# A hybrid decoder layer on one core: clamped decays, sample outer products and wide products of the mixer scan moved between ScalarE, VectorE and GpSimd

## Chip, core and metric

The kernel runs on one core of a Trainium2 chip. The metric is the device time of one execution in microseconds; of several executions the median counts. The profile is one further execution, recorded by the hardware profiler, with its own time and its own span (first to last instruction).

## What is computed

One layer in fp32, 512 prompt tokens and 8 sample tokens (520 columns, width 1024): a half-step SwiGLU feed-forward, a mixer, a second half-step feed-forward, a final norm. The changed lines lie in the mixer. Cut to what they compute:

```python
# prompt: Mamba-2 scan in chunks of 256, 16 heads of 64, 2 groups, state 128
seg = acum[:, :, :, None] - acum[:, :, None, :]
Lm = exp(where(mask, seg, -inf))                 # decays inside a chunk
y_diag = einsum('bclsg,bclsgr,bcsgrp->bclgrp', CB, Lm, xdt)
decay_end = exp(acum[:, :, -1:] - acum)
states = einsum('bclgn,bclgr,bclgrp->bcgrpn', Bc, decay_end, xdt)
S_next = S * exp(acum[:, :, -1]) + states        # between chunks
y_off = einsum('bclgn,bcgrpn,bclgr->bclgrp', Cc, S_enter, exp(acum))
# sample: one token per sequence, 8 sequences, a state of their own
S_new = exp(dt * A) * S0 + (dt * x) outer B
y = S_new . C
# beside it: the short gated convolution
y_sc = sc_b * causal_conv3(sc_c * sc_h)
```

## The kernel before

Activations lie transposed, channels on the 128 partitions and the 520 tokens in the columns, as two halves of 260. Every fp32 product is made of three matmuls of rounded parts (hi with hi, hi with lo, lo with hi), so each block of weights that lands in a `raw` buffer is split: ScalarE copies it to `hi` (L148), VectorE subtracts to get `lo` (L149). `project()` multiplies one block of 128 columns of the input projection: 48 matmuls at L205.

The mixer has three stages. First twelve calls of `conv` (project, width-4 convolution, Silu). Then eight calls of `short(j)`, the gated convolution: three projections each (product with `rr` at L970, product at L975, convolution L979, tail columns on GpSimd L980 to L986, the wide product with `r` at L987, last product L991). Between the projections `pump()` advances two generators: `scan` four times in a round of `short`, `sample` three times. Last come the gate projections and the output projection.

`scan` takes for each of 2 groups, 2 chunks (`i`) and 2 quarters (`q`, four heads) one load of decays (`s0<-scr`, 128 x 1024, L866): eight loads in all. From it come, where `i` is 1, `ce` (exp on ScalarE L870, times C on GpSimd L871), then the clamped differences `s1` (L874, four of 128x128) and `s0` (L877, four of 128x256) on VectorE, exp on ScalarE (L878, L879), then `xd` and `xe` from transposed x (L890, L892, two each), the masks (L893, L894), the matmuls that use them (L904 to L908), the output (L910) and the state (L916, and at `i` = 1 GpSimd's L920 and VectorE's L922).

`sample` has sixteen steps (2 groups, 2 halves of the sequences, 4 blocks `j`). A step loads the state `st` (two buffers, L951), scales it on ScalarE (L953, four of 128x128), makes the outer product `up` in one buffer, `place[2]` (GpSimd L955; in the profile its name is `xs`), adds it (GpSimd L956), stores the state (L957), multiplies by C and reduces (VectorE L958, L960) and adds to x (L961).

Every engine works through its own queue in order. The order in each queue is laid down ahead of time by a planner that runs over the program with estimated costs and takes, of what is ready, what stands first in the program. All loads and stores of this stage are issued from SyncE's queue, in order too.

Of the kernel before, what the change touches and what calls it, by code (L numbers as in the profile page):

```python
# [10 lines left out]
F32 = mybir.dt.float32  # L11
F32R = mybir.dt.float32r
AF = mybir.ActivationFunctionType
ALU = mybir.AluOpType
AX = mybir.AxisListType

P = 128
# [9 lines left out]
HD = 64  # L27
NG = 2
NS = 128
# [644 lines left out]
def mixer(c, o, x, nxt, nx2):  # L674
    nc, tc, a = c.nc, c.tc, c.a
    V, S, G, PE = c.V, c.S, c.G, c.PE
# [9 lines left out]
    with ExitStack() as c0:  # L686
# [28 lines left out]
        place = [t[:, :SEQ].rearrange("p (b n) -> p b n", n=NS) for t in (xst[0][:, 6], xst[0][:, 7], xst[1][:, 6])]  # L715
# [3 lines left out]
        dt = mx.tile([P, NT, NH], F32, name="dt")  # L719
        acs = mx.tile([P, NCH, NH], F32, name="acs")  # L720
# [121 lines left out]
        def scan(sp):  # L842
            states = {}
            for g in range(NG):
                Bt, Ct = xs[8 + g], xs[10 + g]
                for i in range(NC2):
                    l0 = i * 2 * P
                    both, sec = slice(l0, l0 + 2 * P), slice(l0 + P, l0 + 2 * P)
                    blk = [slice(l0, l0 + P), sec]

                    pcb = c.bank()
                    PE.matmul(pcb[:, :2 * P], Bt[:, blk[0]], Ct[:, both], start=True, stop=True)
                    PE.matmul(pcb[:, 2 * P:3 * P], Bt[:, blk[1]], Ct[:, sec], start=True, stop=True)
                    cbm = sp.tile([P, 3 * P], F32, tag="cbm", name="cbm")
                    V.tensor_tensor(cbm, pcb[:, :3 * P], tri.rearrange("p t l -> p (t l)"), op=ALU.mult)
                    pbt = c.bank()
                    for b in range(2):
                        PE.transpose(pbt[:, b * P:(b + 1) * P], Bt[:, blk[b]], idn)
                    btk = sp.tile([P, 2, P], F32, tag="btk", name="btk")
                    S.copy(btk.rearrange("p b n -> p (b n)"), pbt[:, :2 * P])  # L860
                    for q in range(2):
                        hs = slice(g * 8 + q * 4, g * 8 + q * 4 + 4)
                        js = [g * 4 + q * 2, g * 4 + q * 2 + 1]

                        s0 = sp.tile([P, 4, 2 * P], F32, tag="s0", name="s0", bufs=2)
                        nc.sync.dma_start(s0, scr[hs, both].unsqueeze(0).broadcast_to([P, 4, 2 * P]))  # L866
                        s1 = sp.tile([P, 4, P], F32, tag="s1", name="s1", bufs=2)
                        if i:
                            ce = sp.tile([P, 4, 2 * P], F32, tag="ce", name="ce")
                            S.activation(ce, s0, AF.Exp)  # L870
                            G.tensor_tensor(ce, ce, Ct[:, both].unsqueeze(1).broadcast_to([P, 4, 2 * P]), op=ALU.mult)  # L871
                        for h in range(4):
                            hc = g * 8 + q * 4 + h
                            V.tensor_scalar(s1[:, h], s0[:, h, P:], acs[:, 2 * i + 1, hc:hc + 1], 0.0, op0=ALU.subtract, op1=ALU.min)  # L874
                        for h in range(4):
                            hc = g * 8 + q * 4 + h
                            V.tensor_scalar(s0[:, h], s0[:, h], acs[:, 2 * i, hc:hc + 1], 0.0, op0=ALU.subtract, op1=ALU.min)  # L877
                        S.activation(s0, s0, AF.Exp)  # L878
                        S.activation(s1, s1, AF.Exp)  # L879
                        yield  # L880

                        px = c.bank()
                        for b in range(2):
                            for n, j in enumerate(js):
                                PE.transpose(px[:, (2 * b + n) * P:(2 * b + n + 1) * P], xs[j][:, blk[b]], idn)
                        xd = sp.tile([P, 2, 4, HD], F32, tag="xd", name="xd")
                        xe = sp.tile([P, 2, 4, HD], F32, tag="xe", name="xe")
                        for b in range(2):
                            t = 2 * i + b
                            V.tensor_tensor(xd[:, b], px[:, b * 2 * P:(b + 1) * 2 * P].rearrange("p (h d) -> p h d", d=HD),  # L890
                                            dt[:, t, hs].unsqueeze(2).broadcast_to([P, 4, HD]), op=ALU.mult)
                            V.tensor_tensor(xe[:, b], xd[:, b], dec[:, t, hs].unsqueeze(2).broadcast_to([P, 4, HD]), op=ALU.mult)  # L892
                        V.tensor_tensor(s0, s0, cbm[:, :2 * P].unsqueeze(1).broadcast_to([P, 4, 2 * P]), op=ALU.mult)  # L893
                        V.tensor_tensor(s1, s1, cbm[:, 2 * P:].unsqueeze(1).broadcast_to([P, 4, P]), op=ALU.mult)  # L894
                        yield
                        py = c.bank()
                        sin = states.get((g, q))
                        for n in range(2):
                            for step in range(3 if i else 2):
                                for h in (2 * n, 2 * n + 1):  # L900
                                    rows = slice((h % 2) * HD, (h % 2 + 1) * HD)
                                    full = py[rows, n * 2 * P:(n + 1) * 2 * P]
                                    if step == 0:
                                        PE.matmul(full, xd[:, 0, h, :], s0[:, h, :], start=True, stop=False)  # L904
                                    elif step == 1:
                                        PE.matmul(py[rows, n * 2 * P + P:(n + 1) * 2 * P], xd[:, 1, h, :], s1[:, h, :], start=False, stop=not i)
                                    else:
                                        PE.matmul(full, sin[:, h * HD:(h + 1) * HD], ce[:, h, :], start=False, stop=True)  # L908
                        for n, j in enumerate(js):
                            V.scalar_tensor_tensor(xs[j][:, both], xs[j][:, both], par("dsk", j), py[:, n * 2 * P:(n + 1) * 2 * P],  # L910
                                                   op0=ALU.mult, op1=ALU.add)
                        yield

                        pst = c.bank()
                        for b in range(2):
                            PE.matmul(pst[:, :2 * P], btk[:, b], xe[:, b].rearrange("p h d -> p (h d)"), start=b == 0, stop=b == 1)  # L916
                        sn = sp.tile([P, 2 * P], F32, tag=f"st{i}{q}", name="sn")
                        if i:
                            tm = sp.tile([P, 2 * P], F32, tag="tm", name="tm")
                            G.tensor_tensor(tm.rearrange("p (h d) -> p h d", d=HD), sin.rearrange("p (h d) -> p h d", d=HD),  # L920
                                            cd[:, i, hs].unsqueeze(2).broadcast_to([P, 4, HD]), op=ALU.mult)
                            V.tensor_tensor(sn, pst[:, :2 * P], tm, op=ALU.add)  # L922
                            nc.sync.dma_start(o["sp"][g][:, q * 2 * P:(q + 1) * 2 * P], sn)
                        else:
                            S.copy(sn, pst[:, :2 * P])
                        states[g, q] = sn
                        yield


        def sample(sd):  # L930
            pbc = c.bank()
            for n in range(4):
                PE.transpose(pbc[:NB, n * NS:(n + 1) * NS], xs[8 + n][:, SEQ:], idn)
            HB = NB // 2
            bcs = place[2][:NB]
            V.tensor_copy(bcs.rearrange("b t n -> b (t n)"), pbc[:NB])
            scb = c.dram.tile([4, NB, NS], F32, name="scb")
            nc.sync.dma_start(scb.rearrange("t b n -> b t n"), bcs)
            for g in range(NG):
                for k in range(2):  # L940
# [5 lines left out]
                    for j in range(g * 4, g * 4 + 4):  # L946
# [2 lines left out]
                        G.tensor_tensor(xd, xb, ddc[:, j, 0, bs], op=ALU.mult)  # L949
                        st = sd.tile([P, HB, NS], F32, tag="st", name="st", bufs=2)  # L950
                        nc.sync.dma_start(st, a["ssm0"][j][:, bs])  # L951
                        for b in range(HB):
                            S.activation(st[:, b], st[:, b], AF.Copy, scale=ddc[:, j, 1, k * HB + b:k * HB + b + 1])  # L953
                        up = place[2]
                        G.tensor_tensor(up, bb, xd.unsqueeze(2).broadcast_to([P, HB, NS]), op=ALU.mult)  # L955
                        G.tensor_tensor(st, st, up, op=ALU.add)  # L956
                        nc.sync.dma_start(o["ss"][j][:, bs], st)  # L957
                        V.tensor_tensor(up, st, cc, op=ALU.mult)  # L958
                        ys = sd.tile([P, HB], F32, tag="ys", name="ys", bufs=2)
# [7 lines left out]
        def short(j, pump):  # L967
# [16 lines left out]
            for k in range(1, SW):  # L984
                G.tensor_scalar(tmp, ssv[:, j, k], w[k], None, op0=ALU.mult)
                G.tensor_tensor(t1[:, SEQ:], t1[:, SEQ:], tmp, op=ALU.add)  # L986
            G.tensor_tensor(t1, t1, r, op=ALU.mult)  # L987
            pump()
            pbx = project()
            y = ytp.tile([P, T], F32, tag=f"yt{j}", name=f"yt{j}")  # L990
# [144 lines left out]
```

## Time and profile before

| | |
|---|---|
| median of three timed executions | 1176.18 us (1172.96 to 1177.44) |
| the profiled execution | 1172.36 us, its span 1170.6 us |
| mean granted TensorE clock | 0.988 of full speed |
| busy share of the span | TensorE 96%, VectorE 74%, ScalarE 44%, GpSimd 19% |

The profile calls the engines PE (TensorE matmul), PEld (its weight loads), DVE (VectorE), ACT (ScalarE), POOL (GpSimd) and SP (SyncE; a q behind a name is its queue). A row of the timeline merges like instructions that follow each other; their durations overlap by some tens of nanoseconds, so four of them can take less than four times one. Names of tiles are those of the program; several tiles that share a buffer have the name of the first.

### The profile page before, as it was taken

The numbers are of one execution on the slowest core, as the hardware profiler recorded it, in microseconds if no ns is written. First come the engines' busy times: TensorE is split into PE (matmuls) and PEld (weight loads), VectorE is DVE, ScalarE is ACT, GpSimd is POOL, SyncE is SP. The second block draws the span as 40 slices with busy tenths as digits, with TensorE's granted clock in tenths as the row PEclk, the third lists the DMA queues.
The fourth block names the chain that finished last, engine by engine and source line by source line (L and its number), as shares of the span: only waits on it lengthen the run. The fifth ranks groups of instructions, "written<-read, shape, count | busy, mean of one in ns | idle before, by whom it ended". The sixth has DMA issues, their size and how long they took to land.

```text
span 1170.6 us, 21766 instructions
## 1 busy us (share of the span) xinstructions
PE 1123.9 (96%) x9119; PEld 1101.7 (94%) x9119; DVE 871.6 (74%) x1279; ACT 514.4 (44%) x731; POOL 224.6 (19%) x301
## 2 busy tenths in 40 slices
PE   8999999999999999987899999999899999999995
PEld 7989999999999999976799999999799999999994
DVE  7987787778766687788876576348787777786855
ACT  5553444444436574334332344334554444444442
POOL 4000000000003567566643222120000000000002
PEclk9999999999999999999999999999999999999998
DMA  6213322332324433465442322331132223323233
GB/s 199 94 50 113 113 100 66 111 136 77 113 64 135 119 110 97 138 191 164 160 133 79 96 90 72 110 109 50 60 113 91 86 89 110 113 100 112 78 87 74
DMA packets 47434, 122.97 MB, mean 105 GB/s; under 512 B 9384, under 2 KB 19784, under 8 KB 41832
## 3 DMA queue, kind: packets, MB, share of 16 engines
q1 hardware_dynamic: 47336, 121.58, 31.9%
q8 instruction: 71, 1.16, 0.4%
q14 instruction: 27, 0.22, 0.1%
HBM read 114.43 MB, written 7.14 MB: 104 GB/s over the span
## 4 chain that ended last, share of the span: by engine, by line
PE 80%; DVE 6%; POOL 4%; issue 3%; DMA 3%; ACT 3%; SPq 0%; DVEq 0%; POOLq 0%; ACTq 0%
PE pst L221 32%; PE mmt L205 21%; PE auxt L576 20%; PE pst L256 3%; DVE lo L149 2%; POOL xs L955 1%; POOL st L956 1%; ACT hi L148 1%; DMA st<-in_ssm 1%; DMA raw<-in_wu 1%; DMA out_ss<-st 1%; PE auxt L904 0%; DVE y L666 0%; DVE xxl L339 0%; POOL ce L871 0%
## 5 line engine op out<-in xcount | busy, mean ns | idle before, releaser
L148 ACT CAST hi<-raw 128x1024 fp32r<-128x1024 f32 (+3 forms) x218 | 188.5, 869 | 292.8 <-PE mmt L205 105.7
L149 DVE TENSOR_TENSOR lo<-raw,hi 128x1024 fp32r<-128x1024 f32 (+3 forms) x218 | 227.0, 1044 | 60.5 <-ACT hi L148 57.6
L576 PE MATMUL auxt<-hh,hi 128*128 128x260 f32 x704 | 197.7, 283 | 0.8 <-DVE x L577 0.8
L576 PE MATMUL auxt<-hl,hi 128*128 128x260 f32 x704 | 197.5, 283 | 0.0
L576 PE MATMUL auxt<-hh,lo 128*128 128x260 f32 x704 | 194.9, 283 | 0.0
L205 PE MATMUL mmt<-xxh,hi 128*128 128x260 f32 x704 | 146.5, 289 | 0.0
L205 PE MATMUL mmt<-xxl,hi 128*128 128x260 f32 x704 | 143.8, 285 | 0.0
L205 PE MATMUL mmt<-xxh,lo 128*128 128x260 f32 x704 | 143.6, 286 | 0.0
L295 POOL TENSOR_TENSOR acc<-x 128x520 f32<-128x520 f32 x4 | 4.2, 1054 | 697.2 <-DVE x L577 674.9
L576 PEld LDWEIGHTS auxt<-hh,hi 128*128 128x128 f32 x704 | 132.2, 188 | 1.7 <-DVE x L577 0.9
L576 PEld LDWEIGHTS auxt<-hl,hi 128*128 128x128 f32 x704 | 132.5, 188 | 0.0
L576 PEld LDWEIGHTS auxt<-hh,lo 128*128 128x128 f32 x704 | 130.9, 188 | 0.1
L205 PEld LDWEIGHTS mmt<-xxh,hi 128*128 128x128 f32 x704 | 110.2, 190 | 0.6
L205 PEld LDWEIGHTS mmt<-xxl,hi 128*128 128x128 f32 x704 | 110.0, 190 | 0.3 <-issue 0.2
L205 PEld LDWEIGHTS mmt<-xxh,lo 128*128 128x128 f32 x704 | 110.0, 191 | 0.1
L148 ACT CAST hi<-S 128x1024 fp32r<-128x1024 f32 x78 | 80.8, 1050 | 66.6 <-PE pst L221 43.0
L149 DVE TENSOR_TENSOR lo<-S,hi 128x1024 fp32r<-128x1024 f32 x78 | 94.4, 1218 | 19.6 <-ACT hi L148 19.3
L386 ACT ACTIVATE cp<-pst 128x260 f32<-128x260 f32 x117 | 44.8, 386 | 122.0 <-PE pst L221 121.6
L221 PE MATMUL pst<-fxl,hi 128*128 128x260 f32 x320 | 90.2, 283 | 1.4 <-DVE fxl L286 1.4
L221 PE MATMUL pst<-fxh,hi 128*128 128x260 f32 x320 | 90.7, 286 | 0.8 <-ACT hi L148 0.4
L221 PE MATMUL pst<-fxh,lo 128*128 128x260 f32 x320 | 89.2, 283 | 1.0 <-DVE lo L149 1.0
L221 PE MATMUL pst<-fth,hi 128*128 128x260 f32 x304 | 85.7, 285 | 1.3 <-ACT hi L148 0.7
(245 smaller groups left out, 2843.6 us busy)
## 6 DMA issues: line engine op xcount, KB each, us to landing
raw<-in_wi SPq DMA_DIRECT2D x45, 512.0 KB, 3.5
raw<-in_wu SPq DMA_DIRECT2D x22, 1024.0 KB, 4.9
raw<-in_wg SPq DMA_DIRECT2D x21, 1024.0 KB, 4.8
raw<-in_wd SPq DMA_DIRECT2D x48, 384.0 KB, 3.2
raw<-in_wo SPq DMA_DIRECT2D x16, 512.0 KB, 3.8
raw<-in_wd SPq DMA_DIRECT2D x16, 256.0 KB, 2.7
st<-in_ssm SPq DMA_DIRECT2D x16, 256.0 KB, 2.9
s<-scr SPq DMA_DIRECT2D x8, 512.0 KB, 4.7
```

The source lines that it names most:

```text
L148: self.S.copy(hi, src)
L149: self.V.tensor_tensor(lo, src, hi.bitcast(F32), op=ALU.subtract)
L205: self.PE.matmul(ps[:, h, :H2], w[:, k, :], x[:, h * H2:(h + 1) * H2], start=first and n == 0, stop=last and n == 2)
L221: self.PE.matmul(ps[:, :H2], a[:, k, :], b, start=first and k + i == 0, stop=k == n - 1 and i == 2, skip_group_check=True)
L256: self.PE.matmul(ps[h][:, :H2], a, b[:, h * H2:(h + 1) * H2], start=first and n == 0, stop=last and n == 2)
L295: self.G.tensor_tensor(acc, xt, xt, op=ALU.mult)
L386: self.c.S.activation(t, ps[:, :H2], AF.Copy, scale=sign)
L576: PE.matmul(ps[:, :H2], w[:, k, :], v, start=k + n == 0, stop=k == nk - 1 and n == 2)
L955: G.tensor_tensor(up, bb, xd.unsqueeze(2).broadcast_to([P, HB, NS]), op=ALU.mult)
L956: G.tensor_tensor(st, st, up, op=ALU.add)
```

## The change

The clamp min(s - a, 0) becomes relu(a - s) on ScalarE, and the sign goes into the exp behind it. GpSimd's products for `ce`, for the carried state and with `r` go to VectorE. `xd` and `xe` are made by one instruction each instead of two. In `sample`, ScalarE makes the outer product, four instructions with a scale per partition, into one of two buffers, and VectorE scales the state and adds in one pass, four instructions. GpSimd keeps `xd` of the sample (128x4), the tail columns and the small convolution work.

```diff
-  G.tensor_tensor(ce, ce, Ct[:, both]..., op=ALU.mult)
+  V.tensor_tensor(ce, ce, Ct[:, both]..., op=ALU.mult)
   for h in range(4):
-    V.tensor_scalar(s1[:, h], s0[:, h, P:], acs[:, 2*i+1, hc:hc+1], 0.0, op0=ALU.subtract, op1=ALU.min)
+    S.activation(s1[:, h], s0[:, h, P:], AF.Relu, bias=acs[:, 2*i+1, hc:hc+1], scale=-1.0)
   for h in range(4):
-    V.tensor_scalar(s0[:, h], s0[:, h], acs[:, 2*i, hc:hc+1], 0.0, op0=ALU.subtract, op1=ALU.min)
-  S.activation(s0, s0, AF.Exp)
-  S.activation(s1, s1, AF.Exp)
+    S.activation(s0[:, h], s0[:, h], AF.Relu, bias=acs[:, 2*i, hc:hc+1], scale=-1.0)
+  S.activation(s0, s0, AF.Exp, scale=-1.0)
+  S.activation(s1, s1, AF.Exp, scale=-1.0)
...
-  for b in range(2):
-    V.tensor_tensor(xd[:, b], px[...], dt[:, 2*i+b, hs]..., op=ALU.mult)
-    V.tensor_tensor(xe[:, b], xd[:, b], dec[:, 2*i+b, hs]..., op=ALU.mult)
+  V.tensor_tensor(xd, px.rearrange("p (b h d) -> p b h d", b=2, d=HD), wide4(dt), op=ALU.mult)
+  V.tensor_tensor(xe, xd, wide4(dec), op=ALU.mult)
...
-  G.tensor_tensor(tm, sin, cd[:, i, hs]..., op=ALU.mult)
-  V.tensor_tensor(sn, pst[:, :2 * P], tm, op=ALU.add)
+  V.tensor_tensor(sn, sin, cd[:, i, hs]..., op=ALU.mult)
+  V.tensor_tensor(sn, pst[:, :2 * P], sn, op=ALU.add)
...
+  place.append(sd.tile([P, HB, NS], F32, name="up"))
...
+  up = place[2 + j % 2]
   for b in range(HB):
-    S.activation(st[:, b], st[:, b], AF.Copy, scale=ddc[:, j, 1, ...])
-  up = place[2]
-  G.tensor_tensor(up, bb, xd.unsqueeze(2).broadcast_to([P, HB, NS]), op=ALU.mult)
-  G.tensor_tensor(st, st, up, op=ALU.add)
+    S.activation(up[:, b], bb[:, b], AF.Copy, scale=xd[:, b:b + 1])
+  for b in range(HB):
+    V.scalar_tensor_tensor(st[:, b], st[:, b], ddc[:, j, 1, ...], up[:, b], op0=ALU.mult, op1=ALU.add)
...
-  G.tensor_tensor(t1, t1, r, op=ALU.mult)
+  V.tensor_tensor(t1, t1, r, op=ALU.mult)
```

## Rows read from the trace of the kernel before

**Rows 1.** Windows of convolutions, of scan with sample, of the scan's rest.

```profile
360.00:465.00 105.00, 103.06 (x824) 101.40 (x823) 76.07 (x137) 64.64 (x89) 65.68 (x134) 0.97 0.38 116
465.00:600.00 135.00, 118.86 (x943) 111.33 (x942) 116.45 (x179) 51.93 (x98) 86.74 (x97) 0.96 0.49 158
600.00:655.00 55.00, 55.00 (x459) 52.09 (x458) 35.49 (x58) 14.91 (x19) 16.31 (x25) 1.00 0.34 103
```

**Rows 2.** TensorE's waits, 465 to 655 us: total us, times, longest us.

```profile
PE auxt L904 <- DVE xd L890: 11.5, 4, 7.0
```

**Rows 3.** Timeline of TensorE behind its longest wait: start, us, instructions.

```profile
553.94 1.12 PE L904 MATMUL auxt<-s,xd 128*64 128x256 f32 x4 [7.02 <-DVE xd L890]
...
559.40 0.59 PE L205 MATMUL mmt<-xxh,hi 128*128 128x260 f32 x2
```

**Rows 4.** Timeline of VectorE in the 18 us ahead of that matmul.

```profile
536.87 3.74 DVE L877 TENSOR_SCALAR s<-s,acs 128x256 f32<-128x256 f32 x4 [1.28 <-ACT ce L870]
...
541.91 3.02 DVE L877 TENSOR_SCALAR s<-s,acs 128x256 f32<-128x256 f32 x4
...
551.66 0.69 DVE L958 TENSOR_TENSOR xs<-st,xs 128x512 f32<-128x512 f32 x1 [1.36 <-POOL st L956]
```

**Rows 5.** Timeline of GpSimd in the same stretch.

```profile
536.91 2.41 POOL L871 TENSOR_TENSOR ce<-ce,xs 128x1024 f32<-128x1024 f32 x1 [1.89 <-ACT ce L870]
...
542.07 1.08 POOL L955 TENSOR_TENSOR xs<-xs,xd 128x512 f32<-128x512 f32 x1 [2.13 <-DVE ys L960]
```

**Rows 6.** The same clamps on VectorE while GpSimd is idle, timeline.

```profile
595.09 1.13 DVE L877 TENSOR_SCALAR s<-s,acs 128x256 f32<-128x256 f32 x4
...
610.65 0.87 DVE L874 TENSOR_SCALAR s<-s,acs 128x128 f32<-128x128 f32 x4 [2.46 <-DMA s<-scr]
```

**Rows 7.** Groups on VectorE, 465 to 655 us: busy, mean ns, idle before.

```profile
L877 DVE TENSOR_SCALAR s<-s,acs 128x256 f32<-128x256 f32 x24 | 17.4, 785 | 1.3 <-ACT ce L870 1.3
...
L958 DVE TENSOR_TENSOR xs<-st,xs 128x512 f32<-128x512 f32 x16 | 12.1, 754 | 10.2 <-POOL st L956 10.1
...
L893 DVE TENSOR_TENSOR s<-s,cbm 128x1024 f32<-128x1024 f32 x8 | 9.7, 1216 | 1.2 <-ACT s L878 1.2
L874 DVE TENSOR_SCALAR s<-s,acs 128x128 f32<-128x128 f32 x24 | 9.5, 456 | 4.4 <-DMA s<-scr 4.4
L961 DVE SCALAR_TENSOR_TENSOR xs<-xs,pc,ys 128x4 f32<-128x4 f32 x16 | 9.4, 585 | 0.1
...
L890 DVE TENSOR_TENSOR xd<-auxt,dt 128x256 f32<-128x256 f32 x16 | 6.0, 412 | 0.0
L975 DVE TENSOR_TENSOR u<-mmt,t 128x520 f32<-128x520 f32 x8 | 5.5, 693 | 6.2 <-PE mmt L205 6.2
```

**Rows 8.** Two lines of VectorE by themselves: duration ns min/median/max.

```profile
L961 DVE SCALAR_TENSOR_TENSOR xs<-xs,pc,ys x16: 209/498/1119, 483.7 to 595.0; 128x4 f32<-128x4 f32 x16
...
L979 DVE SCALAR_TENSOR_TENSOR t<-u,pc,t x16: 737/747/1776, 475.4 to 644.6; 128x512 f32<-128x512 f32 x16
```

**Rows 9.** Groups on GpSimd, 465 to 655 us, as in Rows 7.

```profile
L955 POOL TENSOR_TENSOR xs<-xs,xd 128x512 f32<-128x512 f32 x16 | 25.5, 1593 | 27.4 <-DVE ys L960 26.6 <-DMA xs<-scb 0.8
L956 POOL TENSOR_TENSOR st<-st,xs 128x512 f32<-128x512 f32 x16 | 21.1, 1318 | 1.1
L987 POOL TENSOR_TENSOR t<-t,r 128x520 f32<-128x520 f32 x8 | 12.4, 1548 | 1.7 <-DVE t L979 1.7
...
L871 POOL TENSOR_TENSOR ce<-ce,xs 128x1024 f32<-128x1024 f32 x4 | 9.6, 2394 | 5.5 <-ACT ce L870 5.5
```

**Rows 10.** Groups on ScalarE, 465 to 655 us, as in Rows 7.

```profile
L953 ACT ACTIVATE st<-st,ddc 128x128 f32<-128x128 f32 x56 | 18.0, 390 | 36.1 <-DMA st<-in_ssm 34.7 <-issue 1.4
...
L977 ACT ACTIVATE t<-u,pc 128x512 f32<-128x512 f32 x8 | 5.8, 721 | 6.4 <-DVE u L975 6.4
```

**Rows 11.** Transfers issued from 465 to 600 us: KB each, us to landing.

```profile
out_ss<-st SPq DMA_DIRECT2D x16, 256.0 KB, 2.6
st<-in_ssm SPq DMA_DIRECT2D x14, 256.0 KB, 2.7
```

More of the change, by code (lines that the diff above doesn't have):

```diff
@@ L870, in scan @@
                             S.activation(ce, s0, AF.Exp)
-                            G.tensor_tensor(ce, ce, Ct[:, both].unsqueeze(1).broadcast_to([P, 4, 2 * P]), op=ALU.mult)
+                            V.tensor_tensor(ce, ce, Ct[:, both].unsqueeze(1).broadcast_to([P, 4, 2 * P]), op=ALU.mult)
                         for h in range(4):
                             hc = g * 8 + q * 4 + h
-                            V.tensor_scalar(s1[:, h], s0[:, h, P:], acs[:, 2 * i + 1, hc:hc + 1], 0.0, op0=ALU.subtract, op1=ALU.min)
+                            S.activation(s1[:, h], s0[:, h, P:], AF.Relu, bias=acs[:, 2 * i + 1, hc:hc + 1], scale=-1.0)
                         for h in range(4):
                             hc = g * 8 + q * 4 + h
-                            V.tensor_scalar(s0[:, h], s0[:, h], acs[:, 2 * i, hc:hc + 1], 0.0, op0=ALU.subtract, op1=ALU.min)
-                        S.activation(s0, s0, AF.Exp)
-                        S.activation(s1, s1, AF.Exp)
+                            S.activation(s0[:, h], s0[:, h], AF.Relu, bias=acs[:, 2 * i, hc:hc + 1], scale=-1.0)
+                        S.activation(s0, s0, AF.Exp, scale=-1.0)
+                        S.activation(s1, s1, AF.Exp, scale=-1.0)
                         yield
@@ L887, in scan @@
                         xe = sp.tile([P, 2, 4, HD], F32, tag="xe", name="xe")
-                        for b in range(2):
[L889 to L892, printed above, removed]
+                        ts = slice(2 * i, 2 * i + 2)
+                        wide4 = lambda t: t[:, ts, hs].unsqueeze(3).broadcast_to([P, 2, 4, HD])
+                        V.tensor_tensor(xd, px.rearrange("p (b h d) -> p b h d", b=2, d=HD), wide4(dt), op=ALU.mult)
+                        V.tensor_tensor(xe, xd, wide4(dec), op=ALU.mult)
                         V.tensor_tensor(s0, s0, cbm[:, :2 * P].unsqueeze(1).broadcast_to([P, 4, 2 * P]), op=ALU.mult)
@@ L918, in scan @@
                         if i:
-                            tm = sp.tile([P, 2 * P], F32, tag="tm", name="tm")
-                            G.tensor_tensor(tm.rearrange("p (h d) -> p h d", d=HD), sin.rearrange("p (h d) -> p h d", d=HD),
+                            V.tensor_tensor(sn.rearrange("p (h d) -> p h d", d=HD), sin.rearrange("p (h d) -> p h d", d=HD),
                                             cd[:, i, hs].unsqueeze(2).broadcast_to([P, 4, HD]), op=ALU.mult)
-                            V.tensor_tensor(sn, pst[:, :2 * P], tm, op=ALU.add)
+                            V.tensor_tensor(sn, pst[:, :2 * P], sn, op=ALU.add)
                             nc.sync.dma_start(o["sp"][g][:, q * 2 * P:(q + 1) * 2 * P], sn)
@@ L951, in sample @@
                         nc.sync.dma_start(st, a["ssm0"][j][:, bs])
+                        up = place[2 + j % 2]
                         for b in range(HB):
-                            S.activation(st[:, b], st[:, b], AF.Copy, scale=ddc[:, j, 1, k * HB + b:k * HB + b + 1])
-                        up = place[2]
-                        G.tensor_tensor(up, bb, xd.unsqueeze(2).broadcast_to([P, HB, NS]), op=ALU.mult)
-                        G.tensor_tensor(st, st, up, op=ALU.add)
+                            S.activation(up[:, b], bb[:, b], AF.Copy, scale=xd[:, b:b + 1])
+                        for b in range(HB):
+                            V.scalar_tensor_tensor(st[:, b], st[:, b], ddc[:, j, 1, k * HB + b:k * HB + b + 1], up[:, b],
+                                                   op0=ALU.mult, op1=ALU.add)
                         nc.sync.dma_start(o["ss"][j][:, bs], st)
```

## The prediction

> **What bounds the kernel now.** I read the page's busy shares first, then TensorE's waits, then windows around them, then the timelines of the engines it waits for. TensorE is the bound nearly everywhere, so only what takes time from it counts. The windows show where the changed lines could matter [rows 1]: with the convolutions it is busy 103 of 105 us, in the last part of the scan 55 of 55, but from 465 to 600 us, where `sample` runs beside `scan`, only 118.86 of 135. That leaves 16.1 us idle. The clock granted there is 0.96 of full: with two levels, 2.4 and 1.2 GHz, a shortfall of 0.04 is 8% of 135 us, or 10.8 us, at the low one, so at most half of it, 5.4 us, is lost besides. The timeline behind the longest wait shows such a piece [rows 3]: the scan's matmuls from 553.94 to 559.40 us follow the wait, and 5.46 us at the low level lose at most 2.7. Between 2.7 and 5.4 I take 3.5. The ceiling of what the change can give back is 16.1 + 3.5 = 19.6 us.
>
> The waits say for whom: L904 waits for VectorE's `xd` (L890) four times, 11.5 us in all, 7.0 at the longest [rows 2]. VectorE is busy 116.45 of these 135 us [rows 1] and stands another 10.1 us waiting for GpSimd's L956 [rows 7]: it is full, and its queue reaches `xd` late.
>
> Its timeline ahead of the longest wait shows what fills it [rows 4]. Four clamps L877 take 3.74 us, and a second four 3.02; with GpSimd idle four take 1.13 [rows 6]. GpSimd was at the same time in L871 for 2.41 us, then in L955 [rows 5]. So a wide GpSimd instruction holds VectorE's. That made 2.61 + 1.89 us, and with the wait of 1.36 for L956 [rows 4] 5.9 of the 7.0 us.
>
> **The change part by part**, in VectorE time of 465 to 655 us, where six of the eight decay loads and all sixteen sample steps are.
>
> Removed. The clamps: 17.4 + 9.5 = 26.9 us [rows 7]; free they would take 6 x (1.13 + 0.87) = 12.0 [rows 6], so 14.9 of it is being held. The wait for L956: 10.1 us [rows 7], since VectorE now adds the state itself. L961 takes 9.4 us for sixteen [rows 7], its shortest 0.209 [rows 8], so 9.4 - 3.3 = 6.1 is being held. The wide products that leave GpSimd are 25.5 + 21.1 + 12.4 + 9.6 = 68.6 us [rows 9] of its 86.74 + 16.31 = 103 [rows 1], two thirds, and I let two thirds of 6.1 go, 4.1. `xd` and `xe` were 32 instructions of 0.412; sixteen of double width at the 0.693 of L975, which reads PSUM too, make 11.1 in place of 13.2 [rows 7], 2.1 less. Together 43.2 us.
>
> Added. Sixty-four scale-and-add instructions of 128x128. The trace has none; the same operation takes 0.209 us for 4 columns and 0.737 for 512 [rows 8], which bound them between 13.4 and 47.2 us. On the line between the two, 128 columns take 0.209 + 124 x 0.528 / 508 = 0.338, and 64 make 21.6; I take that, as one operation should grow evenly. The product with `r`: 8 x 0.693 = 5.5. `ce`: 4 x 1.216 (L893, equal in shape) = 4.9. The carried state: 4 x 0.412 = 1.6 [rows 7]. Together 33.6 us.
>
> Relief: 43.2 - 33.6 = 9.6 us, from -16.0 (all at 0.737) to 17.8 (all at 0.209). Rows of like instructions overlap: 24 of L877 at 0.785 would be 18.8, and 17.4 are busy [rows 7], 0.06 each. The new rows of four have 48 such places: 2.9 more. So VectorE gains about 12.5 us in a stage where it was the one that was late.
>
> Moved to ScalarE. For each load four relus of 128 columns, at 0.390 by L953, and four of 256, between that and the 0.721 of L977 for 512 [rows 10], 0.50 on the line: 3.6 us a load, 21.4 for six. ScalarE is busy 51.93 of 135 us [rows 1]; the outer product replaces the scaling of the state one for one, and the eight scalings that ran ahead of this stage (64 less 56) come into it, 3.1. That makes 76 of 135, so I cost it at nothing, its idle time being the cover. Were that gone, the `hi` copies behind the relus would be late by up to 3.6 us a load. The other two loads fall among the convolutions: 7.2 us more on 64.64 of 105, nothing again, 7.2 at worst.
>
> For the relus the row and the Trainium skill pull apart. Its page "ScalarE: Activation LUTs", section "Rules for kernel authors", says to give relu, max and min to VectorE. By its rule the clamps would stay: 2.0 us a load there against 3.6. What VectorE takes with GpSimd beside it is 26.9 / 6 = 4.5 a load, and by that the sum is better with ScalarE.
>
> Waits that change places. The four adds of a sample step wait on VectorE for the load of `st`; it was ScalarE, with 34.7 us of such waits [rows 10]. Behind them in VectorE's queue stand `lo` and `xd`, for which TensorE waits. A buffer's round is store 2.6, load 2.7 [rows 11] and adds 1.4, or 6.7, so two buffers allow a step each 3.4 us, and 135 us for sixteen give each 8.4. The load should then be there, and I cost this at 0.5, as two or three of sixteen may be short by some tenths. The product with `r` now waits on VectorE for GpSimd's tail columns. There GpSimd waited 1.7 us over the eight for VectorE's L979 [rows 9], so the tail was done no later; from nothing to 8 x 1.55, I take nothing. SyncE's queue has as many transfers as before, and its stores wait for one engine less.
>
> **Sum.** 12.5 - 0.5 = 12 us of the ceiling of 19.6. Against the profiled execution, 1172.36 us with its span of 1170.6, that is 1160.4. The median of the runs is 3.8 above it, and I count from that: 1176.2 - 12 = 1164.
>
> **Rivals.** (a) VectorE stays full. If the new instruction costs the 0.412 of a 128x256 product and doesn't overlap, relief is 9.6 - 4.8 = 4.8 us: 1171. For it: two thirds of GpSimd's time gone is not all, and its small instructions still hold VectorE. Against it: L961's shortest is half of 0.412 [rows 8].
>
> (b) The relus lengthen the way from the load to the masks. If L893 and L894 come later by the 1.6 us more than free clamps, six times, 9.6 of the 12 go: 1174. By the rule in the Trainium skill's page "ScalarE: Activation LUTs", section "Rules for kernel authors", it would come out so. Against it: the clamps do not run free now.
>
> (c) The planner, given other costs, lays the queues so that TensorE meets `xd` as late as before. The order is then the cause, not the holding: 1176, give or take 5. For it: 10 us of slack in an engine do not help an instruction that stands behind the wrong one. Against it: 5.9 of 7.0 us were traced to GpSimd.
>
> (d) Slower: VectorE inherits ScalarE's waits for `st`. From 12.5 of the 34.7 us on, all relief is gone; with half of them, 17.4, it is 1181, with all 1198. For it: an engine in order passes its wait on to everything behind. Against it: the round of 6.7 us for two steps.
>
> **Chances.** The forecast 0.60, its own range 1157 to 1169; (a) 0.12, (b) 0.08, (c) 0.10, (d) 0.10. I take 0.5%, 5.9 us, as what the runs can tell from nothing, since the three shown spread over 4.5. Faster than that is the forecast with half of (a), 0.06, a quarter of (b), 0.02, and 0.03 of (c): 0.71. Within it: the rest of (a) and (b), 0.12, and 0.05 of (c): 0.17. Slower: (d) and 0.02 of (c): 0.12. The range runs from the ceiling, 1156.6, less a spread of 1.6, to 1179, which takes in (a), (b) and most of (c), and leaves out (d).
>
> **What would show it.** In the changed profile TensorE should be busy more than 125 of the stage's time for the same matmuls, and its waits for L890 under half of 11.5 us. L961 should come near 0.21 us, the adds near 0.34, and ScalarE's relus near 0.39 and 0.50. GpSimd's busy time between 465 and 655 us should fall from 103 to about 35. VectorE should wait little for `st` or for GpSimd's tail. I would be wrong if VectorE's waits for the loads of `st` go over 12 us, or the adds over 0.5, or if TensorE waits as long as before at another line.

## The result and the profile after

The changed kernel takes 1157.1 us (median of four, 1155.4 to 1158.34) against 1174.94 before (now also of four): ratio 0.9847, interval 0.9827 to 0.9867. That is 17.8 us less, where 12 were forecast; 1164 was forecast, with 1155 to 1179 as the range. The two profiled executions have spans of 1170.6 and 1153.6 us.

Windows of the changed kernel over the same three stretches as [rows 1]; the columns are the stretch, its length, busy us and instructions of TensorE, its weight loads, VectorE, ScalarE and GpSimd, then granted clock, DMA share and GB/s:

```profile
360.00:465.00 105.00, 102.18 (x840) 100.42 (x839) 70.41 (x120) 70.32 (x99) 63.74 (x133) 1.00 0.38 116
465.00:600.00 135.00, 131.28 (x1082) 125.21 (x1080) 119.42 (x225) 73.11 (x158) 34.09 (x63) 1.00 0.56 177
600.00:655.00 55.00, 55.00 (x461) 52.86 (x460) 33.86 (x46) 21.02 (x28) 10.62 (x17) 1.00 0.28 88
```

From 465 to 600 us TensorE is now idle for 3.7 us, where it was 16.1, and its clock there went from 0.96 to 1.00, the full level. VectorE is busier than before, 119.4 us against 116.45. The stage itself can be measured from the scan's first matmul (L852) to its last (L916, now L915):

```profile
L852 PE MATMUL auxt<-xs x8: 378/379/380, 464.6 to 595.7; 128*128 128x256 f32 x8
...
L915 PE MATMUL auxt<-xe,btk x32: 377/379/484, 480.4 to 632.7; 128*128 128x256 f32 x32
```

464.6 to 632.7 is 168.1 us. Before it ran from 465.0 to 650.0, 185.0. So 16.9 of the 17.0 us by which the spans differ come from this stage. Its windows, before and after, say what they consist of:

```profile
465.00:650.00 185.00, 168.86 (x1359) 158.45 (x1357) 150.04 (x232) 64.89 (x113) 103.05 (x122) 0.97 0.45 142
464.60:632.70 168.10, 164.38 (x1359) 156.15 (x1357) 140.50 (x252) 84.02 (x172) 39.88 (x76) 1.00 0.50 158
```

TensorE's idle time fell from 16.1 to 3.7 us, 12.4 less, and the same matmuls kept it busy for 164.4 us in place of 168.9, 4.5 less. The convolutions' clock also rose, 0.97 to 1.00, but TensorE was idle longer there (2.8 us against 1.9), and the stage began only 0.4 us sooner.

TensorE's waits between 360 and 760 us; the 11.5 us for `xd` [rows 2] are 0.5 now:

```profile
PE auxt L915 <- DVE xe L891: 1.1, 1, 1.1
PE auxt L885 <- ACT btk L860: 1.0, 1, 1.0
PE auxt L931 <- DVE cbm L855: 0.9, 1, 0.9
PE auxt L903 <- DVE xd L890: 0.5, 1, 0.5
```

VectorE's groups, 465 to 655 us, as in [rows 7] (L955 is now the add of the state):

```profile
L149 DVE TENSOR_TENSOR lo<-raw,hi 128x1024 fp32r<-128x1024 f32 x28 | 34.1, 1218 | 5.9 <-ACT hi L148 5.2
L979 DVE SCALAR_TENSOR_TENSOR t<-u,pc,t 128x512 f32<-128x512 f32 x16 | 11.9, 746 | 0.1
...
L955 DVE SCALAR_TENSOR_TENSOR st<-st,ddc,xs 128x128 f32<-128x128 f32 x32 | 9.7, 346 | 6.1 <-ACT xs L953 5.3 <-DMA st<-in_ssm 0.7
L955 DVE SCALAR_TENSOR_TENSOR st<-st,ddc,up 128x128 f32<-128x128 f32 x32 | 9.7, 346 | 1.3 <-ACT up L953 0.7 <-issue 0.6
...
L871 DVE TENSOR_TENSOR ce<-ce,xs 128x1024 f32<-128x1024 f32 x4 | 4.9, 1216 | 0.0
L961 DVE SCALAR_TENSOR_TENSOR xs<-xs,pc,ys 128x4 f32<-128x4 f32 x16 | 3.3, 214 | 0.0
```

The adds take 0.346 us each (0.338 was estimated). L961 fell from 0.585 to 0.214, near its shortest before, 0.209 [rows 8]. From 465 to 640 us no group of VectorE's varies by more than 6% from its shortest to its longest any more, so nothing there is held. It does wait for ScalarE's outer product, 5.3 + 0.7 us; for the load of `st` it waits 0.7.

On GpSimd the small columns remain [rows 9], and on ScalarE the relus stand beside the outer products [rows 10]:

```profile
L985 POOL TENSOR_SCALAR tmp<-ssv,pc 128x8 f32<-128x8 f32 x14 | 14.8, 1054 | 1.4
L986 POOL TENSOR_TENSOR t<-t,tmp 128x8 f32<-128x8 f32 x16 | 7.2, 450 | 1.3
```

```profile
L877 ACT ACTIVATE s<-s,acs 128x256 f32<-128x256 f32 x24 | 10.3, 496 | 0.1
L953 ACT ACTIVATE xs<-xs,xd 128x128 f32<-128x128 f32 x32 | 10.2, 390 | 10.6 <-DMA xs<-scb 6.4 <-DVE ys L960 4.2
...
L874 ACT ACTIVATE s<-s,acs 128x128 f32<-128x128 f32 x24 | 7.8, 390 | 16.4 <-DMA s<-scr 16.4
```

The relus cost what was forecast, 0.390 and 0.496 us, but ScalarE waits 16.4 us in front of them for the decays' loads. The timeline of ScalarE shows what stands behind such a wait:

```profile
511.57 0.99 ACT L874 ACTIVATE s<-s,acs 128x128 f32<-128x128 f32 x3 [6.83 <-DMA s<-scr]
512.46 1.26 ACT L953 ACTIVATE xs<-xs,xd 128x128 f32<-128x128 f32 x4
...
514.60 1.03 ACT L148 CAST hi<-raw 128x1024 fp32r<-128x1024 f32 x1
...
516.71 0.35 ACT L860 COPY btk<-auxt 128x256 f32<-128x256 f32 x1
```

An outer product, a `hi` copy and `btk` come after the 6.83 us. VectorE's add started at 512.89 after an idle 2.50 us that the product ended, and TensorE's L885 at 517.11 after 0.98 that `btk` ended.

### The profile page after: what moved, and what is told of

Its sections match the earlier page's. It is cut to its first block, busy times and chain, and to the rows that moved or that the text cites. A ratio compares the mean times of both kernels' runs of the same rounds, so it can differ in the third digit from the quotient of the medians.

```text
span 1153.6 us, 21775 instructions
## 1 busy us (share of the span) xinstructions
PE 1116.7 (97%) x9119; PEld 1095.4 (95%) x9119; DVE 854.1 (74%) x1279; ACT 538.0 (47%) x797; POOL 158.9 (14%) x253
## 3 DMA queue, kind: packets, MB, share of 16 engines
q1 hardware_dynamic: 47336, 121.58, 32.4%
## 4 chain that ended last, share of the span: by engine, by line
PE 75%; DVE 9%; DMA 6%; ACT 5%; issue 2%; POOL 2%; SPq 1%; DVEq 0%; ACTq 0%; POOLq 0%
PE pst L221 32%; PE auxt L576 20%; PE mmt L205 17%; PE pst L256 4%; DVE lo L149 2%; DMA s<-scr 2%; ACT hi L148 1%; DMA raw<-in_wu 1%; DMA out_ss<-st 1%; DVE st L955 1%; DVE cv L830 1%; DMA st<-in_ssm 1%; ACT s L874 0%; DVE r L313 0%; PE auxt L915 0%
## 5 line engine op out<-in xcount | busy, mean ns | idle before, releaser
L149 DVE TENSOR_TENSOR lo<-raw,hi 128x1024 fp32r<-128x1024 f32 (+3 forms) x218 | 222.5, 1023 | 69.8 <-ACT hi L148 66.6
L149 DVE TENSOR_TENSOR lo<-S,hi 128x1024 fp32r<-128x1024 f32 x78 | 94.4, 1218 | 19.2 <-ACT hi L148 18.7
```

The source lines that it names most:

```text
L149: self.V.tensor_tensor(lo, src, hi.bitcast(F32), op=ALU.subtract)
```

## The experiments

Theory H: a wide GpSimd instruction holds VectorE's, whichever stands next, and the change gains by taking such instructions away. Theory L: only the sum of VectorE's work counts. Theory C: the gain is the shorter chain of a sample step (a second buffer, no GpSimd in it).

**One part of the change alone, on the kernel before.** `relu_only` has the ScalarE clamps only:

```diff
-  V.tensor_scalar(s0[:, h], s0[:, h], acs[...], 0.0, op0=ALU.subtract, op1=ALU.min)
+  S.activation(s0[:, h], s0[:, h], AF.Relu, bias=acs[...], scale=-1.0)
...                                          # the same for s1, and scale=-1.0 in the exps
```

> The kernel before with the clamps alone moved to ScalarE as relus. Theory H (a wide GpSimd instruction holds VectorE's, whichever stands next): GpSimd's 68.6 us of wide products stay, so the holding passes from the clamps to other instructions of VectorE (L961, L979 and L149 grow longer than before), the wait for L956 stays near 10 us, and about half of the 17 us is gained: 1164 to 1170. Theory L (only the sum of VectorE's work counts): 26.9 us leave VectorE and nothing is added, more than the whole change relieves, so all of the gain: 1155 to 1159.

1168.16 us, ratio 0.9941 (0.992 to 0.9961). The time is as H said, and the holding passed on, though only in part where H put it. L961 grew from 0.585 to 0.921, and the wait for L956, which was to stay near 10.1, went to 16.1. L979 and L149, which were to grow too, fell to 0.810 and 1.320; the masks grew instead (L893 1.216 to 1.329). VectorE's groups, 465 to 655 us:

```profile
L961 DVE SCALAR_TENSOR_TENSOR xs<-xs,pc,ys 128x4 f32<-128x4 f32 x16 | 14.7, 921 | 0.3
...
L958 DVE TENSOR_TENSOR xs<-st,xs 128x512 f32<-128x512 f32 x16 | 12.1, 756 | 16.1 <-POOL st L956 16.1
```

`sample_only` has the sample part only (its second buffer lies in the square's scratch tile, idle in this stage):

```diff
-  S.activation(st[:, b], st[:, b], AF.Copy, scale=ddc[...])
-  G.tensor_tensor(up, bb, xd...broadcast_to([P, HB, NS]), op=ALU.mult)
-  G.tensor_tensor(st, st, up, op=ALU.add)
+  S.activation(up[:, b], bb[:, b], AF.Copy, scale=xd[:, b:b + 1])
+  V.scalar_tensor_tensor(st[:, b], st[:, b], ddc[...], up[:, b], op0=ALU.mult, op1=ALU.add)
```

> The kernel before with the sample part alone changed (outer product on ScalarE, scale-and-add on VectorE, a second buffer for the product). Theory H: 46.6 of GpSimd's 68.6 us of wide products and the wait of 10.1 us for L956 go, clamps run near their free 1.13 and 0.87 us a load except beside L871 and L987; two thirds of the gain: 1160 to 1166. Theory L: 19 to 22 us are added to VectorE and 10 us of waiting leave it, the clamps stay at 26.9, so no gain: 1174 to 1180.

1156.39 us, 0.9847 (0.9815 to 0.9879): all of the gain by itself, more than H said, against L. Its window:

```profile
465.00:600.00 135.00, 132.75 (x1098) 127.01 (x1097) 127.23 (x266) 58.34 (x112) 45.46 (x78) 1.00 0.54 174
```

`wide_only` has `ce`, the carried state and the product with `r` on VectorE:

```diff
-  G.tensor_tensor(t1, t1, r, op=ALU.mult)
+  V.tensor_tensor(t1, t1, r, op=ALU.mult)
...                                          # the same for ce and the carried state
```

> The kernel before with only the products for ce, the carried state and r moved from GpSimd to VectorE. Theory H: 25 us of GpSimd's wide work go, a third of the holding, some 8 to 10 us, against 12 us of work added to VectorE: no change, 1171 to 1178. Theory L: 12 us more on a full engine, 1180 to 1188.

1167.38 us, 0.9935 (0.9912 to 0.9957). Faster, where H expected no change and L a loss, so a miss for both: VectorE got more work (121.58 us busy from 465 to 600, 116.45 before), and TensorE was idle for 9.0 us in place of 16.1.

**One part of the change undone.** `no_sample` keeps relus, VectorE's products and the fused `xd` and `xe`, with `sample` as before.

```diff
-  S.activation(up[:, b], bb[:, b], AF.Copy, scale=xd[:, b:b + 1])
-  V.scalar_tensor_tensor(st[:, b], st[:, b], ddc[...], up[:, b], op0=ALU.mult, op1=ALU.add)
+  S.activation(st[:, b], st[:, b], AF.Copy, scale=ddc[...])
+  G.tensor_tensor(up, bb, xd...broadcast_to([P, HB, NS]), op=ALU.mult)
+  G.tensor_tensor(st, st, up, op=ALU.add)
```

> The changed kernel with the sample part as before (GpSimd makes and adds the outer product, one buffer); relus, VectorE's products and the fused xd and xe stay. Theory H: 46.6 us of wide GpSimd work and the wait for L956 stay, 22 are gone; with the clamps off VectorE it has room, 1162 to 1168. If the parts simply added (6.9 for the relus, 7.7 for the products), 1160.

1170.73 us, 0.9967 (0.9948 to 0.9985): a miss for both figures. The two parts that gained 6.9 and 7.7 us alone gain some 4 together, with the fused `xd` and `xe` besides. The windows, of 465 to 600 us and of the stage from its first L852 to its last L915, are the plainest case against L. VectorE is busy 140.59 us of the stage, where the changed kernel has 140.50, yet the stage lasts 181.1 us and not 168.1, and TensorE is idle for 12.2. VectorE's waits at the sample step, 9.9 us for GpSimd's add against 6.7 in the changed kernel, account for 3 of these 13 us at most.

```profile
465.00:600.00 135.00, 122.85 (x976) 116.23 (x975) 111.97 (x150) 66.72 (x141) 76.89 (x100) 0.96 0.53 168
464.50:645.60 181.10, 168.95 (x1357) 159.42 (x1356) 140.59 (x188) 82.48 (x164) 82.89 (x114) 0.97 0.47 147
```

`no_relu` keeps all but the clamps, which go back to VectorE; `no_relu_again` is the same file beside the changed kernel, `after_again`, in one session.

```diff
-  S.activation(s0[:, h], s0[:, h], AF.Relu, bias=acs[...], scale=-1.0)
+  V.tensor_scalar(s0[:, h], s0[:, h], acs[...], 0.0, op0=ALU.subtract, op1=ALU.min)
```

> The changed kernel with the clamps back on VectorE. Theory H: nothing wide is left on GpSimd, so the clamps run free, 2.0 us a load, 12 us more on VectorE in the 135 us of scan with sample, where it is busy 119: full again but not held; 2 to 6 us of the gain go: 1159 to 1163. Theory L: VectorE's 12 us come back as 12 us: 1169. The rule of the page ScalarE: Activation LUTs (clamps belong on VectorE) would have it at 1157 or under.

> The changed kernel with the clamps back on VectorE, once more. If the clamps on ScalarE cost something once nothing wide runs on GpSimd (TensorE waited 3.7 us in the scan with them and not at all without): 1150 to 1154, its ratio below that of the changed kernel beside it. If the 5 us between them was chance: 1155 to 1159.

> The changed kernel once more, on the same chip as the one with the clamps on VectorE: 1155 to 1159 by every theory.

1151.93 us, 0.9815 (0.9787 to 0.9844), then 1152.22, 0.9823 (0.9804 to 0.9843); the changed kernel beside the second 1155.19, 0.9849 (0.9831 to 0.9867). The intervals against the kernel before overlap, but the single runs do not: those without relus lie at 1150.39 to 1154.56 and 1151.15 to 1153.43, those with them at 1155.4 to 1158.34 and 1154.67 to 1156.01. So the relus cost 3 to 5 us, where H expected the clamps on VectorE to cost 2 to 6: a miss for H in its sign. The planner also lays the queues in another order without them, and no run separates the two. The window of `no_relu` has no idle time of TensorE at all, with VectorE 127 us busy, and the clamps run at their free price (the second window is the stage):

```profile
465.00:600.00 135.00, 135.00 (x1120) 129.42 (x1119) 127.44 (x268) 59.55 (x114) 38.93 (x66) 1.00 0.55 177
464.20:627.90 163.70, 163.70 (x1358) 155.95 (x1357) 147.43 (x296) 67.39 (x121) 43.55 (x74) 1.00 0.50 161
```

```profile
L149 DVE TENSOR_TENSOR lo<-raw,hi 128x1024 fp32r<-128x1024 f32 x28 | 34.1, 1218 | 1.7 <-ACT hi L148 1.1
...
L955 DVE SCALAR_TENSOR_TENSOR st<-st,ddc,xs 128x128 f32<-128x128 f32 x32 | 9.8, 344 | 1.7 <-ACT xs L953 1.7
...
L877 DVE TENSOR_SCALAR s<-s,acs 128x256 f32<-128x256 f32 x24 | 7.3, 346 | 0.0
...
L874 DVE TENSOR_SCALAR s<-s,acs 128x128 f32<-128x128 f32 x24 | 5.4, 279 | 3.4 <-DMA s<-scr 3.4
```

**The buffer.** `two_up` gives the kernel before a second buffer for the outer product; `one_up` takes it from the changed kernel.

```diff
-  up = place[2]
+  up = place[2 + j % 2]                    # two_up; one_up has it the other way
```

> The kernel before with a second buffer for the outer product of sample and nothing else. Theory H: GpSimd does the same wide work, so the holding stays: 1171 to 1178. Theory C: GpSimd's next product no longer waits for VectorE's reduction (26.6 us of such waits before), and half or more of the 17 us is gained: 1158 to 1167.

> The changed kernel with one buffer for the outer product in place of two. Theory H: nothing holds VectorE, so little changes, 1156 to 1160. Theory C: ScalarE's product waits for VectorE's reduction each step and VectorE for the product: 1164 to 1172.

1172.64 us, 0.999 (0.9972 to 1.0008), and 1158.95, 0.9853 (0.9811 to 0.9896), each within what H expected. No effect of the buffer shows either way, and C, as far as it rests on it, falls.

**Holding put back.** `held` adds idle work to the changed kernel that changes no output; `beside` is the same work tied to the step:

```diff
+  for _ in range(2):                       # per sample step, over a scratch tile of zeros
+      G.tensor_tensor(idle, idle, idle, op=ALU.mult)                   # held
+      G.tensor_tensor(idle, idle, xd...broadcast_to(...), op=ALU.mult) # beside
```

> The changed kernel with idle work added: two products of 128x512 on GpSimd at each of the sixteen sample steps, over a scratch tile that nothing reads. Theory H (a wide GpSimd instruction holds VectorE's that read two tensors or clamp): no dependence is added, but 32 x 1.05 = 34 us of wide work are back, half of what was removed; L961 and L979 grow longer again, TensorE waits for VectorE again, 1161 to 1168. Theory C (what was removed is the chain of a sample step through one buffer and through GpSimd): the chain is unchanged, so 1155 to 1159.

1166.7 us, 0.9941 (0.9917 to 0.9965), which lies in H's range for another reason. The planner put all of it ahead of the scan, where nothing had to be waited for: GpSimd is busy 89.96 of the convolutions' 105 us, TensorE 97.66, and the scan's own L961 stays at 0.217. It tells nothing on the scan.

> The changed kernel with idle work beside the scan: two products of 128x512 on GpSimd at each sample step, over a scratch tile, reading that step's xd so that they can't run ahead of it. Theory H: 14 x 2 x 1.05 = 29 us of wide work are back beside the scan; VectorE's L149, L961, L979 and the adds grow longer there, and 4 to 10 us are lost: 1161 to 1167. If the gain came from the shorter chain of a sample step alone: 1155 to 1159.

1168.35 us, 0.9955 (0.9936 to 0.9974): 13 us slower than the changed kernel in the same session, and 1.4 above H's range. The window, the idle work, TensorE's wait, and the adds by group (0.346 in the changed kernel) and by shortest, median and longest:

```profile
465.00:600.00 135.00, 123.76 (x1003) 117.98 (x1002) 128.54 (x213) 70.71 (x151) 66.88 (x98) 0.97 0.52 165
```

```profile
L952 POOL TENSOR_TENSOR idle<-idle,xd 128x512 f32<-128x512 f32 x28 | 35.9, 1282 | 1.6
```

```profile
PE auxt L903 <- DVE xd L890: 8.2, 3, 4.6
```

```profile
L959 DVE SCALAR_TENSOR_TENSOR st<-st,ddc,xs 128x128 f32<-128x128 f32 x32 | 17.9, 601 | 2.4 <-ACT xs L957 2.4
L959 DVE SCALAR_TENSOR_TENSOR st<-st,ddc,up 128x128 f32<-128x128 f32 x32 | 15.2, 517 | 0.0
```

```profile
L959 DVE SCALAR_TENSOR_TENSOR st<-st,ddc,xs x32: 336/351/1199, 483.2 to 579.4; 128x128 f32<-128x128 f32 x32
L959 DVE SCALAR_TENSOR_TENSOR st<-st,ddc,up x32: 336/341/1198, 485.8 to 582.8; 128x128 f32<-128x128 f32 x32
```

36 us of GpSimd work that nothing reads lengthen the adds from 19.4 to 33.1 us, and TensorE waits 8.2 us for `xd` again. By the trace, the 29 adds that overlap one of these products take 0.821 us on average, the other 35 take 0.342. L149 stays at 1.232 and the convolution at 0.744, both of which H expected to grow.

The planner's order is not the cause. Between 435 and 690 us VectorE and ScalarE run the same instructions as in the changed kernel, in the same order, one by one. Nor is it that GpSimd's own results come late: VectorE waits 2.4 us for the outer product, less than the 6.0 of the changed kernel, and not at all for GpSimd. Of the 14.5 us between the profiled spans (1168.7 and 1154.2), the stage makes 8.8 (177.7 against 168.9); 4.3 lie ahead of it, where the clock was lower in this execution (0.95 from 360 to 465 us against 0.98), and are not shown to come from the holding.

`beside_clamp` puts the same work into the kernel with the clamps on VectorE:

```diff
-  S.activation(s0[:, h], s0[:, h], AF.Relu, bias=acs[...], scale=-1.0)
+  V.tensor_scalar(s0[:, h], s0[:, h], acs[...], 0.0, op0=ALU.subtract, op1=ALU.min)
...
+      G.tensor_tensor(idle, idle, xd...broadcast_to(...), op=ALU.mult)
```

> The same idle work beside the kernel with the clamps on VectorE. Theory H: the clamps are held too, L877 well over its free 0.35 us; VectorE was busy 127 of 135 us without being held, so now it is late: 1160 to 1168, at least as much slower than its own base as the other. If holding is harmless where the planner's order is good: 1150 to 1154.

1168.61 us, 0.9964 (0.9942 to 0.9987), 16.4 slower than its base, again with VectorE's and ScalarE's order unchanged. Here the stage makes 16.1 (179.8 against 163.7) of the 17.1 us between the profiled spans. L877 grows from 0.346 to 0.466, L961 from 0.214 to 0.501, and TensorE waits 9.1 us for `xd`.

## Why the prediction was right, point by point

- **Place and ceiling.** The place was right: 16.9 of 17.0 us come from the stage. The ceiling of 19.6 was low: `no_relu` runs the stage in 163.7 us (464.2 to 627.9), 21.3 less than before. The idle 16.1 us are all back there, and the other 5.2 are shorter busy time. In the kernel before, TensorE's clock was at its lower level, 0.50 or 1.2 GHz, in two stretches of the stage; the first begins inside the longest wait [rows 3]:

```profile
552.10:558.80 6.70, 4.86 (x25) 2.96 (x26) 6.70 (x12) 3.30 (x7) 5.68 (x9) 0.50 0.51 137
582.90:586.10 3.20, 3.20 (x18) 2.23 (x18) 3.20 (x7) 1.05 (x2) 2.84 (x6) 0.50 0.31 76
```

TensorE was busy 8.06 us there, so the low level cost about 4.0, an estimate from these rows, near the 3.5 taken. What the remaining 1.2 of the 5.2 us consists of stays open.
- **Holding.** That a wide GpSimd instruction holds VectorE's is shown by `beside`, which adds nothing but such instructions (and, ahead of the stage, the clearing of their tile) and leaves the order of VectorE and ScalarE as it was. The Trainium skill, page "SBUF — State Buffer", section "SBUF: two separate sides", has GpSimd and VectorE, where its instruction has two inputs from SBUF, share a port pair that the first to start keeps for its whole instruction. Here the trace agrees for the adds: they take up to 1.199 us beside products of 1.04. Not every instruction of VectorE's is drawn out, as L149 and the convolution show. The prediction's reading of the second four clamps was short of a row: L955's 1.08 us [rows 5] can't make 1.89, but the add stood right behind it:

```profile
543.23 1.29 POOL L956 TENSOR_TENSOR st<-st,xs 128x512 f32<-128x512 f32 x1
```

- **What GpSimd keeps.** The step that let a third of the holding stay was wrong. L961 went to 0.214, L979 from 0.872 to 0.746, L149 from 1.367 to 1.218: 6.1 of VectorE for the first, where 4.1 were taken, and 2.1 and 24 x 0.149 = 3.6 for the others, which were not counted. GpSimd pays: L985 went from 0.586 to 1.054, and it is busy 34.09 + 10.62 = 45 us, not 35.
- **Adds and products.** 0.346 for 0.338, 19.4 us for the 64; the product with `r` 0.696 for 0.693, `ce` 1.216 for 1.216, the carried state 0.416 for 0.412. These were right. So was the overlap of the adds, 2.7 us (64 x 0.346 less 19.4) for 2.9, though 24 clamps in fours have 18 such places and not the 24 counted.
- **Waits that change places.** The load of `st` was right at 0.7 us for 0.5, so rival (d) did not come about. What was missed is ScalarE's outer product, 6.0 us of VectorE's waiting; with the clamps on VectorE (`no_relu`) it is 1.7.
- **The relus on ScalarE, costed at nothing.** Wrong, and the runs show 3 to 5 us. Its idle time was counted as cover, with 76 of 135 us busy, and 73 were. But ScalarE's queue stands still for the loads of the decays, 16.4 us, with `hi` copies and outer products behind. In `no_relu` VectorE waits 1.7 us for these products in place of 6.0 and 1.1 for the copies in place of 5.2, and TensorE not at all. By the rule of the Trainium skill's page "ScalarE: Activation LUTs", section "Rules for kernel authors", the clamps stay on VectorE; without holding, the runs agree with it, 1152 against 1155 and 1157. While GpSimd is wide they do not: `relu_only` gained 6.9 us. Rival (b), priced at 1174, was right in sign only.
- **The sum.** What it was for came out: 12 us were forecast from VectorE's relief, and TensorE's idle time fell by 12.4. The term that was mis-sized is the clock. The ceiling had 3.5 us for it, the sum nothing, and 4.5 came back as shorter busy time. The two make 16.9 of the 17.0 us between the spans; the medians differ by 17.8.
- **Luck in the sum.** The relief was right because two misses cancelled: 7.7 us more of holding went (6.1 - 4.1 + 2.1 + 3.6), and 6.0 of waiting for ScalarE came. VectorE's busy time and the waits at its adds fell from 160.1 (150.04 + 10.1) to 147.2 us (140.50 + 6.7), 12.9 less. That a microsecond of VectorE gives one of TensorE does not hold elsewhere. By the same count `no_sample` has 9.6 us less (140.59 + 9.9) and gives TensorE 4.0; `no_relu` has 11.0 less (147.43 + 1.7) and gives 16.1. That held instructions come at times that the planned order does not know, and so make `xd` late, is seen in `beside`, where the order is unchanged; for the other runs it is argued.
- **Rivals (a) and (c)** did not come about: VectorE stayed just as full and TensorE no longer waited for it, and TensorE's order is nearly the one of before. VectorE's order did change: of 209 instructions that both kernels run from 430 to 690 us, 168 stand in the same order. What that is worth no run shows.

What stays open: how much of the sample part's gain is the holding and how much that VectorE no longer waits for GpSimd's add (10.1 us). With 36 us of wide work `beside` loses 13 us, of which its trace shows 8.8 in the stage, and `beside_clamp` 16.4, of which 16.1. In `sample_only` 24 us of wide work remain (10.5 + 10.3 + 3.3) and the adds are still held, at 0.436 and 0.407; `no_relu`, without that work and with the fused `xd` and `xe`, is 4.5 us faster, though their single runs overlap. So the price of holding need not be in proportion to the work.

The fastest version is that with the clamps on VectorE and everything else as changed: 1152.2 us, 0.9823 of the kernel before.

## What to carry to other kernels

Where an order is laid down ahead, look for instructions whose time varies from case to case (0.35 and 2.6 us for one clamp here), and ask what ran beside them; moving the partner that holds them was worth more than making the held ones fewer. An engine's free time does not make a move to it free: what counts is what its new instructions wait for, and what stands behind them. Judge the parts of a change one by one, since here one part made up the whole gain and another took some back.

## What was not expected of the hardware

GpSimd's instructions of 128x8 do not lengthen VectorE's to any extent that shows (L961 at 207 to 218 ns over all sixteen), while they are themselves drawn out, L985 from a shortest of 0.305 us to a mean of 1.05 and once to 3.80. The holding goes both ways, but in these runs only wide GpSimd work lengthens VectorE's instructions, and not all of them. And VectorE at 127 of 135 us busy kept TensorE from no work at all.
